# A Griffin-style encoder layer on one core: two score tiles of the short sequence in one PSUM buffer

## The chip, the cores and the metric

The kernel runs on one core of a Trainium2 chip. The metric is the device time of one launch, in microseconds (us), as the median of several runs. A core has five engines that run side by side: PE (TensorE, matrix multiplications; its weight loads are shown apart as PEld), DVE (VectorE), ACT (ScalarE), POOL (GpSimd) and SP (SyncE, which here only issues DMAs). PE writes its results to PSUM, a small memory of eight banks; a bank holds 512 fp32 numbers in each of 128 partitions, the output of one matmul of 512 columns. ACT and DVE read PSUM; POOL works on SBUF, the large working memory.

## The reference

One encoder layer is applied to two sequences with the same weights: `x_prompt` with 1024 tokens (the long sequence) and `x_sample` with 512 tokens (the short one). Cut to what matters here:

```python
z = xn @ w_in                          # xn = RMSNorm(x); split into q, k, v of A and B, two gates
# branch A: 8 query heads, 2 key/value heads, head width 64, every token sees every token
s = jnp.einsum('bqkgd,bskd->bkgqs', qi, k, preferred_element_type=jnp.float32) * scale
p = jax.nn.softmax(s, axis=-1)
o = jnp.einsum('bkgqs,bskd->bqkgd', p.astype(v.dtype), v)
# branch B: attention to a neighbourhood on a token grid, with a bias
merged = sigmoid(ga) * (o_a @ w_proj_a) + sigmoid(gb) * (o_b @ w_proj_b)
h = h + merged @ w_out
h = h + square(relu(RMSNorm(h) @ w_mlp_up)) @ w_mlp_down      # then a final RMSNorm
```

All of it is in fp32. The kernel keeps the precision by splitting a number into a high and a low part, each in a faster format of the matmul, and by adding two or three matmuls for one product.

## The kernel before

`run` does the token mixer of one sequence: first the short one (trunk 0, T = 512, NT = 4 blocks of 128 tokens, NB = 1 block of 512), then the long one (trunk 1, T = 1024, NB = 2). `mlp` then does the MLP for both. In the first 1050 us or so of the profile the mixers run, in the rest the MLP.

Branch A of a sequence is done in two passes, `g` = 0 and 1, one for each key/value head. In a pass, `phR` projects, normalises and rotates queries and keys (L630 to L711), and `phA` (L714 to L787) does the attention of four query heads. A *unit* of `phA` is one head and 512 queries; the short sequence has 4 units in a pass, and a unit has 4 score tiles j = 0 to 3 of 128 queries each. For one score tile, `s_tile` (L718)

- takes a PSUM buffer `s` (L723) and puts the scores into it: for each 512 keys one matmul with the keys' high part (L726) and one with the low part (L727);
- takes the negated maximum of each row on DVE (L729), and on ACT the exp of the scores with the row sum (L732): the last read of the PSUM buffer;
- divides: reciprocal on DVE (L734), scaling on POOL (L735).

The loop at L756 then goes through the key blocks kc = 0 to NT-1 of a unit: PE transposes the four tiles' probabilities of that key block into one PSUM bank (L769), ACT copies out the high part (L774), DVE makes the low part (L775), and two key blocks later PE multiplies with the values (`pv`, L745 and L746). The next unit's score tiles are written into the same loop: in the short sequence tiles 0 and 1 at kc = 0, tile 2 at kc = 1, tile 3 at kc = 2 (L777 to L780). `fill.pull` (L782) puts pieces of other work between: matmuls of the gate projection (`gate`, L409, through `mm3`, L190 to L193; tiles `gps`).

PSUM is shared by two pools. `pmm` has four buffers of one bank (`mm`, L93); `pbig` has two buffers of two banks each, 1024 columns (`big`, L96). Score tiles take `big` buffers. In the long sequence a score tile has 1024 columns and fills one; in the short sequence it has 512 columns, so `[:, :T]` uses one bank of the two. Other users of `big` are `transpose_tile` (L273: eight transposes into one buffer, L277; then for each of its two banks a copy on ACT, L287, and a subtraction on DVE, L293) and branch B's `s_unit` (L919). `s_unit` takes one buffer for two score tiles, one for each bank: for x = 0 and 1 two matmuls (L949), a reduction on DVE that reads the bank (L951), the exp on ACT (L955) and a scaling on POOL (L959).

All waits are set by the framework from what each instruction reads and writes and from when a buffer of a pool comes free. It also sets the order of the instructions on each engine, from its own plan of the run: earlier lines go first as far as they are planned to be ready, and operations marked `tc.keep_in_program_order` keep their place. So matmuls of `s_tile` and of the gate stand mixed on PE. On each engine the instructions then run in the order set.

Of the kernel before, what the change touches and what calls it, by code (L numbers as in the profile page):

```python
# [61 lines left out]
def encoder(ctx: ExitStack, tc: tile.TileContext, xs, outs, w):  # L62
# [21 lines left out]
    def phase(name, bufs=2):  # L84
        return tc.tile_pool(name=name, bufs=bufs, reuse_waits="tile")
# [7 lines left out]
    def mm(name):  # L93
        return pmm.tile([P, 512], F32, tag="mm", name=name)

    def big(name):  # L96
        return pbig.tile([P, 1024], F32, tag="big", name=name)
# [69 lines left out]
    def bias_row(r):  # L167
        nc.sync.dma_start(biases[r], shifted[:, :, 7 - r : 23 - r, :])
# [228 lines left out]
    def run(tr, nxt, first):  # L397
        N, x, T, NT, NB = tr.N, tr.x, tr.T, tr.NT, tr.NB
# [35 lines left out]
        def finish_o(o, n, dst, pool, nm):  # L434

            t = pool.tile([HD, 512], F32, tag="ot", name=f"ot_{nm}", bufs=1)
            nc.scalar.activation(t[:, :n], o[HD:P, :n], AF.Copy)
            b = pool.tile([HD, 512], F32, tag="os", name=f"os_{nm}", bufs=2)
            nc.vector.tensor_tensor(b[:, :n], o[0:HD, :n], t[:, :n], op=ALU.add)
            nc.scalar.dma_start(dst, b[:, :n])  # L440


        def load_a(g, between=None, then=None, last=None):
            wh, wl, rq = [], [], []
            for kb in range(2):
                wh.append(slot([P, 4, 384], F32R, f"wgh{N}_{g}_{kb}"))
                wl.append(slot([P, 4, 384], F32R, f"wgl{N}_{g}_{kb}"))
                raw = rawp.tile([P, 1024], F32, tag="raw", name=f"rawq{N}_{g}_{kb}")
                rv = raw.rearrange("p (k c) -> p k c", c=256)
                nc.sync.dma_start(  # L450
                    rv,
                    win[kb * 512 : (kb + 1) * 512, 256 * g : 256 * g + 256].rearrange("(k p) c -> p k c", p=P),
                )
                rq.append(rv)
            if between is not None:
                between()
            if then is None:
                for kb in range(2):
                    split(wh[kb][:, :, 0:256], wl[kb][:, :, 0:256], rq[kb])
            else:  # L460
                then([(wh[kb][:, :, 0:256], wl[kb][:, :, 0:256], rq[kb]) for kb in range(2)])
            raw = rawp.tile([P, 1024], F32, tag="raw", name=f"rawkv{N}_{g}")
            rv = raw.rearrange("p (k c) -> p k c", c=P)
            for i, off in enumerate((512 + 64 * g, 640 + 64 * g)):
                nc.sync.dma_start(
                    rv[:, :, 64 * i : 64 * i + 64],
                    win[:, off : off + 64].rearrange("(k p) c -> p k c", p=P),
                )
            if last is not None:
                last()  # L470
            for kb in range(2):
                split(
                    wh[kb][:, :, 256:384],
                    wl[kb][:, :, 256:384],
                    rv[:, kb * 4 : kb * 4 + 4, :],
                    between is not None,
                )
            return wh, wl

        def load_v(g, alloc, pin=False):  # L480
            return load_cols(win, 1792 + 256 * g, 256, f"v{N}_{g}", alloc, pin)

        early = {}
        for g in range(2):
            with phase(f"phR{N}_{g}") as ph:
# [122 lines left out]
                for tt in range(NT):  # L608
                    tb, j = divmod(tt, 4)
                    nm = f"{N}_{g}_{tt}"  # L610
# [103 lines left out]
            with phase(f"phA{N}_{g}") as ph:  # L714
                units = [(h, qb) for h in range(4) for qb in range(NB)]
                PP = {}

                def s_tile(u, j):  # L718
                    h, qb = u
                    nm = f"{N}_{g}_{h}_{qb}_{j}"  # L720
                    q0 = (qb * 4 + j) * P
                    lhs = qT[h % 2][:, h // 2, q0 : q0 + P]
                    s = big(f"s{nm}")[:, :T]  # L723
                    for kb in range(NB):
                        ks = slice(kb * 512, kb * 512 + 512)
                        nc.tensor.matmul(s[:, ks], lhs, kT[:, 0, ks], start=True, stop=False)  # L726
                        nc.tensor.matmul(s[:, ks], lhs, kT[:, 1, ks], start=False, stop=True)  # L727
                    nm_ = sml.tile([P, 1], F32, tag="nm", name=f"nm{nm}")
                    nc.vector.tensor_reduce(nm_, s, axis=AX.X, op=ALU.max, negate=True)  # L729
                    p = ph.tile([P, T], F32, tag="P", name=f"p{nm}", bufs=8)  # L730
                    l = sml.tile([P, 1], F32, tag="l", name=f"l{nm}")
                    nc.scalar.activation(p, s, AF.Exp, bias=nm_, accum_out=l)  # L732
                    rl = sml.tile([P, 1], F32, tag="rl", name=f"rl{nm}")
                    nc.vector.reciprocal(rl, l)  # L734
                    nc.gpsimd.tensor_scalar(p, p, rl, 1.0, op0=ALU.mult, op1=ALU.mult)  # L735
                    PP[u, j] = p

                o_of = {}

                def pv(u, kc, hi, lo):  # L740
                    h, qb = u
                    if kc == 0:
                        o_of[u] = mm(f"o{N}_{g}_{h}_{qb}")
                    o = o_of[u]
                    nc.tensor.matmul(o, vhl[:, kc, :], hi, start=(kc == 0), stop=False)  # L745
                    nc.tensor.matmul(o, vhl[:, kc, :], lo, start=False, stop=(kc == NT - 1))  # L746
                    if kc == NT - 1:
                        r0 = (g * 4 + h) * HD
                        finish_o(o, 512, oad[r0 : r0 + HD, qb * 512 : qb * 512 + 512], ph, f"A{N}_{g}_{h}_{qb}")

                for j in range(4):
                    s_tile(units[0], j)
                    fill.pull(2)
                queue = []
                LAG = 2
                for ui, u in enumerate(units):  # L756
                    h, qb = u
                    if first:
                        bias_row(g * 4 + ui)
                        if g == 0 and ui == 1:  # L760
                            early["a"] = load_a(1)
                        if g == 0 and ui == 2:
                            early["v"] = load_v(1, slot)
                    nxt_u = units[ui + 1] if ui + 1 < len(units) else None
                    sdone = 0
                    for kc in range(NT):
                        pt = mm(f"pT{N}_{g}_{h}_{qb}_{kc}")
                        for j in range(4):
                            nc.tensor.transpose(  # L769
                                pt[:, j * P : (j + 1) * P], PP[u, j][:, kc * P : (kc + 1) * P], ident  # L770
                            )
                        hi = ph.tile([P, 512], F32R, tag="pth", name=f"pth{N}_{g}_{h}_{qb}_{kc}", bufs=3)
                        lo = ph.tile([P, 512], F32R, tag="ptl", name=f"ptl{N}_{g}_{h}_{qb}_{kc}", bufs=3)
                        nc.scalar.activation(hi, pt, AF.Copy)  # L774
                        nc.vector.tensor_tensor(lo, pt, hi.bitcast(F32), op=ALU.subtract)  # L775
                        queue.append((u, kc, hi, lo))
                        if nxt_u is not None:  # L777
                            while sdone < 4 and kc >= ((0, 1, 3, 4) if NB == 2 else (0, 0, 1, 2))[sdone]:
                                s_tile(nxt_u, sdone)
                                sdone += 1  # L780

                        fill.pull(1 if NB == 1 or kc % 4 < 3 else 0)  # L782
                        if len(queue) > LAG:
                            pv(*queue.pop(0))
                fill.drain()
                for item in queue:
                    pv(*item)  # L787
# [55 lines left out]
        with phase(f"phB{N}") as ph:  # L843
# [210 lines left out]
            for i in range(n + LS + LV):  # L1054
                if NB == 1:
                    f = 9 if i < 1 else 5 if i < n - 4 else 6 if i < n else 4 if i == n else 2
                else:
                    f = 0 if i == n - 10 else 5 + (i % 3 > 0) if i < n - 8 else 7
# [37 lines left out]
        with phase(f"phG{N}") as ph:  # L1096
# [25 lines left out]
            for c in range(NC8):  # L1122
# [4 lines left out]
                for tb in range(NB):  # L1127
# [4 lines left out]
                    nm = f"{N}_{c}_{tb}"  # L1132
# [33 lines left out]
            for half in range(2):  # L1166
                wo = wos[half]
                hc = slice(half * 512, half * 512 + 512)
                for tt in range(NT):
                    tb, j = divmod(tt, 4)  # L1170
                    nm = f"{N}_{half}_{tt}"
# [61 lines left out]
                    if half == 1:  # L1233
# [5 lines left out]
                        if nxt is None:  # L1239
# [10 lines left out]
                            if 3 <= tt <= 5:  # L1250
                                j = tt - 3
# [556 lines left out]
    for i, tr in enumerate(trunks):  # L1808
        run(tr, trunks[i + 1] if i + 1 < len(trunks) else None, i == 0)
# [66 lines left out]
```

## Time and profile before

| what | us |
|---|---|
| median of 3 runs | 2132.78 (2132.7 to 2134.22) |
| the profiled execution | 2134.04 |
| its span, first to last instruction | 2132.2 |
| DVE busy | 1473.7 |
| ACT busy | 1114.3 |
| first pass of the short sequence's branch A, score tiles | 52.5 to about 85 |
| second pass, score tiles | 129 to about 161 |

A row of a group reads: line, engine, operation, tiles out<-in, shape, count, then times. Buffer numbers are left out of names, so `ss` is a score tile of branch A, `ps` its probabilities, `pTs` the transposed ones, `sbs` a score buffer of branch B, `ptxs` a buffer of transposed input, `gpss` a gate's sum. In the view of one tile, a row has the shortest, median and longest duration in ns, and the first and last start in us; below it stand the pauses by what ended them (us in total, times). In the timeline, the columns are start, duration, engine, line, operation and tiles; in brackets stands the idle time before it and who ended it. In the table by stretches, x counts instructions, and PEclk is PE's granted clock. A list of waits has engine, tile and line, then who was waited for: us in total, times, the longest.

### The profile page before, as it was taken

What the parts mean: (1) busy time and instruction counts of PE and PEld (TensorE: products, weight loads), DVE (VectorE), ACT (ScalarE), POOL (GpSimd) and SP (SyncE); (2) the same over time, 40 slices, a digit from 0 to 9 for tenths busy, and PEclk for the clock granted to TensorE, in tenths of its full rate; (3) what the DMA queues carried; (4) which work ended last, traced back from release to release, by engine and by line L of the source; (5) the groups of instructions that cost most, each with busy time, mean ns of one, the idle gap of its engine ahead of it and who ended that gap; (6) DMA issues with size and microseconds to landing.
All of it is one profiled execution on the core that took longest, in us unless ns stands there. A gap on an engine that the chain in (4) does not pass through costs nothing. (4 is left out here: it accounts for less than half of the span.)

```text
span 2132.2 us, 31826 instructions
## 1 busy us (share of the span) xinstructions
PE 2114.7 (99%) x10982; PEld 1849.5 (87%) x10982; DVE 1473.7 (69%) x2805; ACT 1114.3 (52%) x2345; POOL 388.2 (18%) x506
## 2 busy tenths in 40 slices
PE   9999999999999999999999999999999999999998
PEld 8888788988898888888888999999999988888887
DVE  6675686777667754656782977778777777759563
ACT  5654664556536644655531566566655643434352
POOL 2232420433233223433300200003000000000000
PEclk9999999999999999999999999999999999999999
DMA  6435567620221132433472666578445799688561
GB/s 187 130 105 171 156 187 242 195 72 30 62 83 53 43 108 85 123 106 108 138 247 101 212 200 193 161 249 210 158 145 159 255 351 341 220 275 281 172 197 70
DMA packets 319578, 350.91 MB, mean 165 GB/s; under 512 B 31160, under 2 KB 255032, under 8 KB 319417
## 3 DMA queue, kind: packets, MB, share of 16 engines
q1 hardware_dynamic: 278071, 279.91, 41.8%
q10 hardware_dynamic: 35666, 51.93, 7.0%
q0 software_dynamic: 5680, 17.04, 2.8%
q8 instruction: 87, 1.43, 0.3%
q14 instruction: 74, 0.61, 0.1%
HBM read 264.85 MB, written 87.88 MB: 165 GB/s over the span
## 5 line engine op out<-in xcount | busy, mean ns | idle before, releaser
L193 PE MATMUL dn<-wd,al 128*128 128x512 f32 (+1 forms) x624 | 242.4, 389 | 0.0
L192 PE MATMUL dn<-wd,ah 128*128 128x512 f32 (+1 forms) x624 | 242.4, 388 | 0.0
L191 PE MATMUL dn<-wd,ah 128*128 128x512 f32 (+1 forms) x624 | 242.4, 388 | 0.0
L1289 ACT ACTIVATE ah<-ar 128x512 fp32r<-128x512 f32 x168 | 104.4, 627 | 203.9 <-PE dn L192 183.3
L1290 DVE TENSOR_TENSOR al<-ar,ah 128x512 fp32r<-128x512 f32 x168 | 115.3, 693 | 77.5 <-ACT ah L1289 65.0
L193 PEld LDWEIGHTS dn<-wd,al 128*128 128x128 f32 x624 | 117.2, 188 | 24.2
L192 PEld LDWEIGHTS dn<-wd,ah 128*128 128x128 f32 x624 | 117.2, 188 | 24.1
L191 PEld LDWEIGHTS dn<-wd,ah 128*128 128x128 f32 x624 | 117.2, 188 | 24.0
L735 POOL TENSOR_SCALAR ps<-ps,rls 128x1024 f32<-128x1024 f32 (+1 forms) x96 | 96.8, 1010 | 215.7 <-DVE rls L734 201.3
L775 DVE TENSOR_TENSOR ptls<-pTs,pths 128x512 fp32r<-128x512 f32 x160 | 107.6, 686 | 37.8 <-ACT pths L774 37.1
L774 ACT ACTIVATE pths<-pTs 128x512 fp32r<-128x512 f32 x160 | 94.1, 598 | 73.7 <-PE pTs L769 71.7
L729 DVE TENSOR_REDUCE nms<-ss 128x1 f32<-128x1024 f32 (+1 forms) x96 | 99.8, 1041 | 24.9 <-PE ss L727 24.4
L176 POOL TENSOR_TENSOR rs_f<-ms_f,mhalf 128x1 f32<-128x1 f32 x6 | 4.0, 666 | 590.7 <-DVE ms_f L172 590.7
L732 ACT ACTIVATE ps<-ss,nms 128x1024 f32<-128x1024 f32 (+1 forms) x96 | 93.2, 972 | 23.8 <-DVE nms L729 19.8
L191 PE MATMUL gpss<-xs_0h,w_gs 128*128 128x512 f32 x256 | 104.7, 409 | 0.3 <-ACT w_gs L180 0.2
L769 PEld LDWEIGHTS pTs<-ident,ps 128*128 128x128 f32 x640 | 78.1, 140 | 28.2 <-POOL ps L735 4.1
L193 PE MATMUL gpss<-xs_0h,w_gs 128*128 128x512 f32 x256 | 101.0, 394 | 0.0
L192 PE MATMUL gpss<-xs_0l,w_gs 128*128 128x512 f32 x256 | 100.8, 394 | 0.0
L769 PE MATMUL pTs<-ident,ps 128*128 128x128 f32 x640 | 98.9, 274 | 1.2 <-DVE ptls L775 0.5
L1289 ACT ACTIVATE A<-S 128x512 fp32r<-128x512 f32 x128 | 76.0, 624 | 30.0 <-DVE S L1352 26.8
L1408 ACT ACTIVATE c<-c 128x384 f32<-128x384 f32 x97 | 50.8, 524 | 69.0 <-DVE c L1407 69.0
L1290 DVE TENSOR_TENSOR A<-S,A 128x512 fp32r<-128x512 f32 x128 | 84.4, 685 | 3.4 <-ACT A L1289 3.4
(344 smaller groups left out, 6402.3 us busy)
## 6 DMA issues: line engine op xcount, KB each, us to landing
ar<-ud SPq DMA_DIRECT2D x120, 512.0 KB
br<-in_w_mlp_down_dram SPq DMA_DIRECT2D x72, 512.0 KB
rawu<-in_w_mlp_up_dram SPq DMA_DIRECT2D x64, 512.0 KB
ud<-c ACTq DMA_DIRECT2D x128, 192.0 KB
raw_gs<-in_w_in_dram SPq DMA_DIRECT2D x32, 512.0 KB
zgs<-sgs ACTq DMA_DIRECT2D x48, 256.0 KB
ud<-cs SPq DMA_DIRECT2D x64, 192.0 KB
raw_os<-in_w_out_dram SPq DMA_DIRECT2D x16, 512.0 KB
```

The lines of the kernel that those rows point to most:

```text
L191: nc.tensor.matmul(out, ah, bh, start=start, stop=False, **kw)
L192: nc.tensor.matmul(out, ah, bl, start=False, stop=False, **kw)
L193: nc.tensor.matmul(out, al, bh, start=False, stop=stop, **kw)
L729: nc.vector.tensor_reduce(nm_, s, axis=AX.X, op=ALU.max, negate=True)
L732: nc.scalar.activation(p, s, AF.Exp, bias=nm_, accum_out=l)
L735: nc.gpsimd.tensor_scalar(p, p, rl, 1.0, op0=ALU.mult, op1=ALU.mult)
L769: nc.tensor.transpose(pt[:, j * P : (j + 1) * P], PP[u, j][:, kc * P : (kc + 1) * P], ident)
L774: nc.scalar.activation(hi, pt, AF.Copy)
L775: nc.vector.tensor_tensor(lo, pt, hi.bitcast(F32), op=ALU.subtract)
L1289: nc.scalar.activation(hi, src, AF.Copy)
L1290: nc.vector.tensor_tensor(lo, src, hi.bitcast(F32), op=ALU.subtract)
L1408: nc.scalar.activation(t, t, AF.Relu)
```

## The change

In branch A of the short sequence (NB = 2 is the long one) two successive score tiles share one buffer: the even tile takes a new `big` buffer and its first 512 columns, the odd one takes the second 512 columns of the same buffer. In the long sequence every tile still takes its own.

```diff
                 units = [(h, qb) for h in range(4) for qb in range(NB)]
                 PP = {}
+                pair = []
 
                 def s_tile(u, j):
...
                     lhs = qT[h % 2][:, h // 2, q0 : q0 + P]
-                    s = big(f"s{nm}")[:, :T]
+                    if NB == 2 or j % 2 == 0:
+                        pair[:] = [big(f"s{nm}")]
+                    s = pair[0][:, :T] if NB == 2 else pair[0][:, j % 2 * 512 : j % 2 * 512 + 512]
                     for kb in range(NB):
                         ks = slice(kb * 512, kb * 512 + 512)
                         nc.tensor.matmul(s[:, ks], lhs, kT[:, 0, ks], start=True, stop=False)
```

`ks` counts within `s`, so it is the same for both halves. The number of instructions of each kind stays as it is.

## The prediction

> **What bounds the kernel now.** I read the page first: the engines, then the chain that ended last.
>
> ```profile
> span 2132.2 us, 31826 instructions
> PE 2114.7 (99%) x10982; PEld 1849.5 (87%) x10982; DVE 1473.7 (69%) x2805; ACT 1114.3 (52%) x2345; POOL 388.2 (18%) x506
> ...
> PE 44%; DVE 0%; issue 0%; ACT 0%; POOLq 0%; POOL 0%; DVEq 0%; ACTq 0%
> ```
>
> PE (matmuls) is busy for 2114.7 of 2132.2 us, and the chain is PE alone. The change removes no matmul, so it can act only through time in which PE stands still: 2132.2 - 2114.7 = 17.5 us in the whole span. How much of it lies where the change is made? The table by stretches has the short sequence's branch A, first pass (52 to 97) and second pass (128 to 170).
>
> ```profile
> core 0: us, PE busy (x) PEld busy (x) DVE busy (x) ACT busy (x) POOL busy (x), PEclk, DMA share, GB/s
> 52.00:97.00 45.00, 43.97 (x219) 34.13 (x218) 33.72 (x69) 31.40 (x66) 11.88 (x16) 1.00 0.46 141
> ...
> 128.00:170.00 42.00, 41.46 (x211) 32.61 (x210) 30.93 (x63) 28.32 (x62) 12.07 (x17) 1.00 0.42 117
> ```
>
> PE is idle there for 1.03 + 0.54 = 1.6 us. Next, the view of the score tile `ss` up to 230 us: its instructions, and the pauses that ended at them or because of them.
>
> ```profile
> L726 PE MATMUL ss<-kTs,qTs x32: 389/476/505, 52.5 to 158.1; 128*128 128x512 f32 x32
> ...
> L729 DVE TENSOR_REDUCE nms<-ss x32: 671/691/693, 54.4 to 159.3; 128x1 f32<-128x512 f32 x32
> L732 ACT ACTIVATE ps<-ss,nms x32: 676/687/705, 55.3 to 160.2; 128x512 f32<-128x512 f32 x32
> ...
>   ACT ps L732: 2.3, 5
> ...
>   PEld ss L726: 1.7, 4
>   PE ss L726: 0.6, 1
> ```
>
> There are 32 score tiles. Their matmuls waited for an exp (L732) five times, 2.3 us in all: 1.7 us is idle time of the weight loader (PEld), 0.6 us of PE itself. That is the wait for a free score buffer. The timeline shows the largest one:
>
> ```profile
> 82.16 0.19 PEld L726 LDWEIGHTS ss<-kTs,qTs 128*128 128x128 f32 x1 [0.81 <-ACT ps L732]
> 82.16 0.50 PE L726 MATMUL ss<-kTs,qTs 128*128 128x512 f32 x1 [0.58 <-ACT ps L732]
> ```
>
> **Removed: the wait for a buffer.** Today tile j of a unit takes the buffer of tile j-2 and waits for that tile's exp. With pairs, tiles 0 and 1 lie in one buffer, 2 and 3 in the other, and a pair takes the buffer of the pair before last, whose exps are a unit old. The five waits go: between 0.6 us (PE's own idle time) and 2.3 us (the loader's added). Does anything take their place?
>
> **Added: tile 1 behind tile 0.** The two halves are different banks, but they are one tile to whoever sets the waits. The kernel already has such a layout: branch B's `s_unit` puts two scores into the two banks of one buffer (L949), each read by a reduction on DVE (L951). The second score reads nothing that the first one's reduction makes, so if waits went by bank, it would not wait. The first and the last of the 48 units, in the timeline:
>
> ```profile
> 184.67 0.42 DVE L951 CUSTOM_DVE_ANT_0 sbss<-sbs,bms 128x256 f32<-128x256 f32 x1 [0.59 <-issue]
> 185.02 0.08 DVE L951 DVE_READ_ACCUMULATOR2_ANT msbs<- 128x1 f32 x1
> 185.16 0.30 PEld L949 LDWEIGHTS sbs<-kBs,qBs 128*128 128x128 f32 x2 [0.37 <-DVE msbs L951]
> 185.16 0.51 PE L949 MATMUL sbs<-kBs,qBs 128*128 128x256 f32 x2
> ...
> 1043.96 0.56 DVE L951 CUSTOM_DVE_ANT_0 sbss<-sbs,bms 128x384 f32<-128x384 f32 x1 [0.30 <-PE sbs L949]
> 1044.44 0.08 DVE L951 DVE_READ_ACCUMULATOR2_ANT msbs<- 128x1 f32 x1
> ...
> 1044.58 0.30 PEld L949 LDWEIGHTS sbs<-kBs,qBs 128*128 128x128 f32 x2 [0.17 <-DVE msbs L951]
> ```
>
> The second score's matmuls start 0.06 us (185.16 - 185.10) or more after the first one's reduction has ended. So it is in 44 of the 48 units; in the other four two scores go out ahead of a reduction, as two units' first scores may, and never more than two. A second place says the same. In `transpose_tile` eight transposes fill a buffer, four to a bank:
>
> ```profile
> 8.58 1.11 PE L277 MATMUL ptxs<-ident,xns 128*128 128x128 f32 x4
> 9.91 1.06 PE L277 MATMUL ptxs<-ident,xns 128*128 128x128 f32 x4
> 11.01 1.09 ACT L287 ACTIVATE xs_0h<-ptxs 128x512 fp32r<-128x512 f32 x2 [2.32 <-PE ptxs L277]
> 12.13 0.69 DVE L293 TENSOR_TENSOR xs_0l<-ptxs,xs_0h 128x512 fp32r<-128x512 f32 x1 [2.72 <-ACT xs_0h L287]
> ```
>
> The first bank is full at 9.69; ACT, idle for 2.32 us, starts reading it at 11.01, when the second bank is full too (10.97). So I take waits to go by tile: after the change tile 1 waits for tile 0's exp, and tile 3 for tile 2's. How long that is, the timeline shows for one tile:
>
> ```profile
> 56.65 0.39 PE L726 MATMUL ss<-kTs,qTs 128*128 128x512 f32 x1
> 56.88 0.39 PE L727 MATMUL ss<-kTs,qTs 128*128 128x512 f32 x1
> 57.30 0.69 DVE L729 TENSOR_REDUCE nms<-ss 128x1 f32<-128x512 f32 x1 [0.38 <-PE ss L727]
> 58.03 0.69 ACT L732 ACTIVATE ps<-ss,nms 128x512 f32<-128x512 f32 x1 [1.30 <-DVE nms L729]
> 58.62 0.19 ACT L732 ACTIVATION_READ_ACCUMULATOR ps<-ss,nms 128x1 f32 x1
> ```
>
> From first matmul to last read: 58.81 - 56.65 = 2.2 us. That is the same chain as today, and there are as many links: two per unit inside it (before, 0 to 2 and 1 to 3; after, 0 to 1 and 2 to 3) and two to the next unit. In the opening of a pass tiles 0 and 2 go out first in place of 0 and 1, and the four exps end when they do now. What changes is how near in the program a link's ends lie. `s_tile` is called at key blocks 0, 0, 1, 2: today's links span one and two key blocks, the new ones none and one. So each of the 16 odd tiles (2 passes x 4 heads x 2) becomes a close link, behind which PE's whole queue stands: the gate matmuls, the transposes (L769), the value products (L745, L746).
>
> **The price of a close link.** No row shows it for branch A, so I bound it by branch B's:
>
> ```profile
> PE sbs L949 <- DVE msbs L951: 1.3, 4, 0.4
> ...
> PEld sbs L949 <- DVE msbs L951: 11.7, 37, 0.9
> ```
>
> By PE's own idle time it is 1.3 / 48 = 0.03 us per link, by both together 13.0 / 48 = 0.27 us; for 16 tiles 0.4 or 4.3 us. Less what is removed, by the same two measures: 0.4 - 0.6 = -0.2 us, or 4.3 - 2.3 = +2.0 us. Idle time of the loader is partly covered by the matmul still running; one row of a close link shows both:
>
> ```profile
> 190.27 0.30 PEld L949 LDWEIGHTS sbs<-kBs,qBs 128*128 128x128 f32 x2 [0.63 <-DVE msbs L951]
> 190.27 0.51 PE L949 MATMUL sbs<-kBs,qBs 128*128 128x256 f32 x2 [0.20 <-DVE msbs L951]
> ```
>
> 0.20 of 0.63, about a third, reaches PE. Counting a third of the loader's pauses (my choice, from this row): added (1.3 + 11.7/3) / 48 x 16 = 1.7 us, removed 0.6 + 1.7/3 = 1.2 us; net **+0.5 us**.
>
> **What hides a later score.** The next unit's first transposes need all four of its probabilities, the last one after POOL's scaling:
>
> ```profile
> 66.90 0.69 POOL L735 TENSOR_SCALAR ps<-ps,rls 128x512 f32<-128x512 f32 x1 [0.33 <-DVE rls L734]
> ...
> 67.58 0.60 PE L769 MATMUL pTs<-ident,ps 128*128 128x128 f32 x4
> ```
>
> They start just as that ends (67.59), so a later tile 3 delays the unit. PE meanwhile does gate matmuls, which have to be done anyway:
>
> ```profile
> L191 PE MATMUL gpss<-xs_0h,w_gs x26: 388/392/475, 51.9 to 90.1; 128*128 128x512 f32 x26
> ```
>
> They last until 90.1 of a pass that ends near 95, and behind them the next pass' projections are ready. I cost the delay at nothing. If the gate matmuls ran out early, the delay itself would show on PE (second rival).
>
> **Sum.** 2134.04 us (the profiled execution; 1.84 us lie around its span) + 0.5 = 2134.5. That execution is 1.3 us above the median of the runs, 2132.78, so the forecast for the median is **2133.3 us**: no change that can be told, since about 0.2%, 4.3 us, is the least that a measurement of this kernel tells from none.
>
> **Rivals.** *Waits go by bank.* Then tile 1 is free at once, the buffer waits go and nothing comes: 2132.78 - 1.2 = 2131.6, at best 2132.78 - 2.3 = 2130.5; still within 0.2%. Against it stand branch B's units and the transposes; for it only that branch B's reader is another instruction than an exp. The Trainium skill ("PSUM — Partial Sum Buffer", "PSUM bank collisions raise a hardware error") has PSUM guarded by bank and quadrant, not by the whole buffer; by that rule tile 1 would need no wait, and the two places above do not agree with it. Chance 0.06.
>
> *Every odd tile stops PE.* Tile 1 is ready in the plan just when tile 0's exp is planned to end; if DVE or ACT is late in fact, PE stops as at 82.16, for 0.58 us, in both passes. 16 x 0.58 = 9.3, less 0.6: +8.7 us, 2141.5. It is over 0.2% from (4.3 + 0.6) / 16 = 0.31 us of PE idle per odd tile. For it: the two links of a unit are closer than today's. Against it: branch B's 48 close links cost 0.03 us of PE each. Chance 0.08, of which 0.07 over 0.2%.
>
> *The order elsewhere shifts.* The order on each engine is planned as a whole, so scores that stand elsewhere may move waits in later stages. Between those stages and now lie 17.5 - 1.6 = 15.9 us of PE idle; a third of it more or less is 5 us (an estimate), 2127.5 to 2138.1. Nothing in the profile points to a side. Chance 0.13: 0.04 faster by over 0.2%, 0.05 within, 0.04 slower.
>
> *The change does nothing at all:* tiles 1 and 2 merely trade places, and the time stays at 2132.8; this lies inside the forecast's case.
>
> **Numbers.** The forecast has 0.73: its bounds are 2132.6 to 2134.8. Range for 8 in 10: 2130.5 (waits by bank at best) to 2136.5 (odd tiles at 0.27 us of PE each: 4.3 - 0.6 = +3.7). Faster by over 0.2%: 0.04, and 0.01 taken from the forecast for what I overlook, 0.05. Slower: 0.07 + 0.04 = 0.11. Same: 0.72 + 0.06 + 0.01 + 0.05 = 0.84.
>
> **What would show it.** In the profile after, in each unit tile 2's first matmul should stand before tile 1's, tile 1's matmul just behind tile 0's exp; idle before L726 put down to the exp should be near 16 x 0.27 = 4 us, mostly PEld's; PE idle in the two passes near 2 us; PE's busy time unchanged. Two scores back to back in one buffer would show waits by bank; over 5 us of PE idle in front of L726 the second rival; equal passes and another time, the third.

## The result, and the profile after

The changed kernel takes 2137.42 us (median of 18 runs, 2135.74 to 2138.33), the kernel before 2133.25 us (18 runs, 2132.43 to 2134.84): a ratio of 1.0019, 95% interval 1.0013 to 1.0025. It is 4.2 us slower, 0.9 us above the top of the predicted range. The profiled execution took 2138.22 us. Its page, with the span, the busy times and the chain:

```profile
span 2135.9 us, 31820 instructions
...
PE 2116.1 (99%) x10982; PEld 1848.8 (87%) x10982; DVE 1474.8 (69%) x2805; ACT 1115.8 (52%) x2345; POOL 389.7 (18%) x506
...
PE 81%; DVE 2%; DMA 2%; issue 1%; ACT 1%; POOL 1%; SPq 0%; ACTq 0%; POOLq 0%; DVEq 0%
```

The span grew by 3.7 us, PE's idle time from 17.5 to 19.8 us. The lines of `phA` have moved down by three: L726 is now L729, the maximum L732, the exp L735, the scaling L738, the value products L748 and L749, the transposes L772, the low part L778.

Where does the time go? A good gauge is an instruction that has the same matmuls in front of it in both kernels. Branch B's first score, right behind the second pass, is one. In the view of its tile `sbs`, the first start stands after the durations; before and after:

```profile
L949 PE MATMUL sbs<-kBs,qBs x64: 279/285/391, 182.7 to 295.3; 128*128 128x256 f32 x64
```

```profile
L952 PE MATMUL sbs<-kBs,qBs x64: 279/284/391, 186.2 to 298.7; 128*128 128x256 f32 x64
```

3.5 us of the 3.7 us are lost by then. 1.1 us of them are lost in the first pass: the matmuls `zs` behind it begin at 94.4 before and at 95.5 after. The table by stretches, from branch A's first score to branch B's first, has the same work in both kernels (the counts differ by one at the edge); before and after:

```profile
52.53:182.72 130.19, 128.62 (x688) 107.16 (x687) 85.17 (x196) 75.19 (x192) 37.76 (x53) 1.00 0.44 132
```

```profile
52.49:186.22 133.73, 130.15 (x687) 106.82 (x686) 86.17 (x196) 75.99 (x192) 38.83 (x53) 1.00 0.43 129
```

PE is idle there for 1.6 us before and 3.6 us after. The other 1.5 us of the loss stand in PE's busy time, though the matmuls are the same. A matmul's row reaches into the next one: rows of 0.39 us start 0.23 us apart. So a pause of up to 0.16 us between two of them does not show as idle time. What holds PE? The view of the score tile `ss` up to 230 us, after:

```profile
L729 PE MATMUL ss<-kTs,qTs x32: 389/476/501, 52.5 to 161.3; 128*128 128x512 f32 x32
...
  DVE nms L732: 13.9, 12
  PE ss L730: 7.7, 9
  ACT ps L735: 0.8, 4
...
  PEld ss L729: 0.8, 4
```

The scores themselves stop PE less than before: pauses behind an exp are 0.8 us (four times, the weight loader alone) instead of 2.3. What has grown is ACT's idle time before an exp, waiting for a maximum: 13.9 us against 5.4 (`DVE nms L729: 5.4, 8` before). The maxima come late. The opening of the first pass, in the timeline of after (the other work of PE left out), shows how:

```profile
55.24 0.69 ACT L735 ACTIVATE ps<-ss,nms 128x512 f32<-128x512 f32 x1 [0.40 <-DVE nms L732]
55.43 0.39 PE L729 MATMUL ss<-kTs,qTs 128*128 128x512 f32 x1
...
55.65 0.39 PE L730 MATMUL ss<-kTs,qTs 128*128 128x512 f32 x1
...
56.56 0.39 PE L729 MATMUL ss<-kTs,qTs 128*128 128x512 f32 x1
...
56.79 0.39 PE L730 MATMUL ss<-kTs,qTs 128*128 128x512 f32 x1
...
57.21 1.29 DVE L732 TENSOR_REDUCE nms<-ss 128x1 f32<-128x512 f32 x2 [1.00 <-PE ss L730]
...
57.94 0.69 ACT L735 ACTIVATE ps<-ss,nms 128x512 f32<-128x512 f32 x1 [1.92 <-DVE nms L732]
```

At 55.24 tile 0's exp starts. At 55.43 PE writes tile 2, complete at 56.04. At 56.56, behind tile 0's exp, it writes tile 1, complete at 57.18. DVE has stood idle for 1.00 us, although tile 2 has been ready since 56.04, because its own order is still 0, 1, 2, 3: tile 1's maximum stands in front. It then does both in one stretch (x2, 1.29 us); ACT, in the same order, idles for 1.92 us. PE's order is now 0, 2, 1, 3 and the readers' is 0, 1, 2, 3: the orders *cross*, and tile 2 waits 1.78 us for nothing that it needs. It is so in every unit of both passes. At three of the six changes of unit, moreover, the next unit's tile 0 goes out ahead of tile 3 (its first matmul at 59.08 against 59.44, 74.94 against 78.03, 137.22 against 137.57), which crosses the orders once more. Summed over the 32 tiles, the time from the end of a score's second matmul to the start of its maximum is 11.9 us before and 31.2 us after. Unit 0's last exp starts at 60.93, against 59.16.

How that reaches PE, the second pass shows in one place:

```profile
158.91 1.26 DVE L732 TENSOR_REDUCE nms<-ss 128x1 f32<-128x512 f32 x2
...
160.09 1.27 DVE L778 TENSOR_TENSOR ptls<-pTs,pths 128x512 fp32r<-128x512 f32 x2
...
160.91 0.63 PE L772 MATMUL pTs<-ident,ps 128*128 128x128 f32 x4 [1.03 <-DVE ptls L778]
```

The maxima of tiles 1 and 2 of the last unit come as one block at 158.91. The low parts stand behind them on DVE, and PE's next transposes wait 1.03 us for the first low part, the last reader of a bank of `pmm`. By lines, from 45 to 180 us (busy time, mean ns, then idle time before and what ended it), before:

```profile
L191 PE MATMUL gpss<-xs_0h,w_gs 128*128 128x512 f32 x64 | 25.9, 404 | 0.1
...
L769 PE MATMUL pTs<-ident,ps 128*128 128x128 f32 x128 | 21.0, 276 | 0.7 <-POOL ps L735 0.3 <-DVE ptls L775 0.2
L726 PE MATMUL ss<-kTs,qTs 128*128 128x512 f32 x32 | 14.4, 451 | 0.7 <-ACT ps L732 0.6
```

and after:

```profile
L191 PE MATMUL gpss<-xs_0h,w_gs 128*128 128x512 f32 x64 | 26.1, 408 | 1.0 <-ACT sgs L430 1.0
...
L772 PE MATMUL pTs<-ident,ps 128*128 128x128 f32 x128 | 22.4, 277 | 2.1 <-DVE ptls L778 1.0 <-POOL ps L738 0.4 <-DVE os_As L439 0.2
L729 PE MATMUL ss<-kTs,qTs 128*128 128x512 f32 x32 | 14.3, 455 | 0.0
...
L748 PE MATMUL os<-pths,vhls 128*128 128x512 f32 x32 | 13.1, 409 | 0.4 <-DVE ptls L778 0.4
```

The idle time in front of scores (0.7 us) is gone. In its place stand 2.1 us in front of transposes, 1.0 us in front of gate matmuls (which wait for the gate's sigmoid on ACT, `sgs`), and 0.4 us in front of value products. That is the idle time alone. Counted from the start of a matmul to the start of the next, and compared with the usual step of its kind (the median before), all of the 3.5 us show: 2.0 us more in front of transposes, 1.2 us of value products, 1.2 us of gate matmuls and 0.2 us of the next projection's transposes, 1.0 us less in front of scores.

### The profile page after: what moved, and what is told of

Same layout as the page of the kernel before. It is cut to its first block, busy times and chain, and to the rows that moved or that the text cites. A ratio compares the mean times of both kernels' runs of the same rounds, so it can differ in the third digit from the quotient of the medians.

```text
span 2135.9 us, 31820 instructions
## 1 busy us (share of the span) xinstructions
PE 2116.1 (99%) x10982; PEld 1848.8 (87%) x10982; DVE 1474.8 (69%) x2805; ACT 1115.8 (52%) x2345; POOL 389.7 (18%) x506
## 4 chain that ended last, share of the span: by engine, by line
PE 81%; DVE 2%; DMA 2%; issue 1%; ACT 1%; POOL 1%; SPq 0%; ACTq 0%; POOLq 0%; DVEq 0%
PE dn L191 7%; PE dn L192 7%; PE dn L193 7%; PE pTs L772 3%; PE gpss L191 3%; PE gpss L193 3%; PE gpss L192 2%; PE ud L191 2%; PE uc L191 2%; PE ud L192 2%; PE uc L192 2%; PE uc L193 2%; PE ud L193 2%; PE ua L191 2%; PE ua L192 2%; PE ua L193 2%
## 5 line engine op out<-in xcount | busy, mean ns | idle before, releaser
L738 POOL TENSOR_SCALAR ps<-ps,rls 128x1024 f32<-128x1024 f32 (+1 forms) x96 | 96.6, 1007 | 221.7 <-DVE rls L737 214.4
L778 DVE TENSOR_TENSOR ptls<-pTs,pths 128x512 fp32r<-128x512 f32 x160 | 107.3, 686 | 37.9 <-ACT pths L777 37.4
L732 DVE TENSOR_REDUCE nms<-ss 128x1 f32<-128x1024 f32 (+1 forms) x96 | 99.4, 1040 | 23.5 <-PE ss L730 22.8
L735 ACT ACTIVATE ps<-ss,nms 128x1024 f32<-128x1024 f32 (+1 forms) x96 | 93.2, 972 | 31.4 <-DVE nms L732 28.9
L772 PEld LDWEIGHTS pTs<-ident,ps 128*128 128x128 f32 x640 | 78.0, 140 | 30.9 <-POOL ps L738 5.7
L772 PE MATMUL pTs<-ident,ps 128*128 128x128 f32 x640 | 100.3, 274 | 2.6 <-DVE ptls L778 1.4
```

The lines of the kernel that those rows point to most:

```text
L772: nc.tensor.transpose(pt[:, j * P : (j + 1) * P], PP[u, j][:, kc * P : (kc + 1) * P], ident)
```

## The experiments

The theory to be tested: **crossed orders**. The tile-level wait makes the plan put tile 2's matmuls ahead of tile 1's, while DVE and ACT keep the order of the program; a score that is ready stands behind one that isn't, the unit's probabilities come later, and PE pays downstream. The rivals: the **close link** (PE itself loses at the wait of tile 1 for tile 0's exp), and the **sharing** itself (that two tiles lie in one buffer, whatever the orders). All kernels were timed in five rounds against the kernel before on the same chip. As 1 to 2 us of a single profile also come from later stages, the table has the time that the profile shows for the two passes, from the first score of branch A to the first score of branch B (130.2 us before).

| kernel | orders cross | median us (before) | ratio, 95% interval | two passes, us |
|---|---|---|---|---|
| the changed kernel | all 8 units | 2137.42 (2133.25) | 1.0019 [1.0013, 1.0025] | +3.5 |
| calls 0, 2, 1, 3 | none | 2134.13 (2133.69) | 1.0000 [0.9991, 1.0009] | +0.3 |
| readers 0, 2, 1, 3 | 2 units | 2136.36 (2133.69) | 1.0012 [1.0003, 1.0021] | +1.3 |
| own buffers, PE crossed | all 8 | 2137.35 (2133.69) | 1.0017 [1.0008, 1.0026] | +2.7 |
| own buffers, readers crossed | all 8 | 2136.30 (2134.17) | 1.0011 [1.0003, 1.0020] | +2.1 |
| sharing in the first pass only | 4 units | 2135.62 (2134.17) | 1.0007 [0.9999, 1.0016] | +1.3 |
| sharing in the second pass only | 4 units | 2135.76 (2134.17) | 1.0007 [0.9998, 1.0016] | +1.6 |
| last tile first | all 8 | 2138.28 (2133.65) | 1.0022 [1.0013, 1.0031] | +5.2 |
| torn on purpose | none | 2133.03 (2133.65) | 0.9996 [0.9987, 1.0005] | -0.5 |

**The sharing kept, the orders made to agree.** The changed kernel, with `s_tile` called for tiles 0, 2, 1, 3; the pairs 0 and 1, 2 and 3 still share.

```diff
-                for j in range(4):
+                CALLS = (0, 2, 1, 3) if NB == 1 else (0, 1, 2, 3)
+                for j in CALLS:
...
-                                s_tile(nxt_u, sdone)
+                                s_tile(nxt_u, CALLS[sdone])
```

> The changed kernel with the tiles of the short sequence called in the order 0, 2, 1, 3; tiles 0 and 1 still share a buffer, 2 and 3 the other. Main theory (queue order): PE writes the scores in the order 0, 2, 1, 3 because tile 1 waits for the exp of tile 0, while DVE and ACT read them in the order 0, 1, 2, 3, so tile 2 stands in PSUM until tile 1 is through; here all three engines have the order 0, 2, 1, 3, and the time goes back to that of before, 2133.3 us within 1 us. Rival link (PE loses at each close wait of tile 1 for tile 0): the wait spans two calls here, as before the change, so 2133.3 us too. Rival sharing (matmuls into one bank of a buffer and reads of its other bank slow each other): nothing is changed, 2137.4 us.

2134.13 us: no loss that can be told, and 0.3 us in the two passes. In its timeline the readers take tile 2 at once:

```profile
54.74 0.40 PE L730 MATMUL ss<-kTs,qTs 128*128 128x512 f32 x1
55.17 0.69 DVE L732 TENSOR_REDUCE nms<-ss 128x1 f32<-128x512 f32 x1 [0.16 <-PE ss L730]
...
55.90 0.69 ACT L735 ACTIVATE ps<-ss,nms 128x512 f32<-128x512 f32 x1
...
56.59 0.39 PE L729 MATMUL ss<-kTs,qTs 128*128 128x512 f32 x1
```

The maximum of 55.17 is tile 2's, 0.03 us behind its second matmul, and the waits from matmul to maximum are back at 12.0 us. The two tiles still share, and tile 1's matmuls (56.59) still come behind tile 0's exp, but nothing is lost. So sharing costs nothing by itself. The waits keep a matmul into one bank of a buffer and a read of its other bank apart here, so what those two would cost each other side by side, no run shows. Nor does this run part the crossing from the close link: with the calls 0, 2, 1, 3 the link lies two calls apart again, as in the kernel before.

**The link kept, the readers' order changed.** `s_tile` is cut in two, the matmuls (`s_mm`) and the readers (`s_rest`). Only the readers of tile 1 are written behind those of tile 2; its matmuls keep their place in the program.

```diff
+                def s_call(u, j):
+                    if NB == 1 and j == 1:
+                        late.append(partial(s_rest, u, j, *s_mm(u, j)))
+                        return
+                    s_tile(u, j)
+                    while late:
+                        late.pop()()
```

> The changed kernel with tile 1's matmuls where they are and only its reads (maximum, exp, scaling) written behind those of tile 2. PE keeps the order 0, 2, 1, 3 and the close wait of tile 1 for the exp of tile 0; DVE and ACT get 0, 2, 1, 3. Queue order: 2133.3 to 2134.5 us. Rival link: 2137 us, as the wait of PE is kept. Rival sharing: 2137.4 us.

About two thirds of the loss in the two passes is gone (1.3 us left of 3.5), the median less: 2136.36 lies above the range expected, and its interval overlaps that of the changed kernel, so by the median alone the two cannot be told apart (the profile puts a further 1.3 us into later stages). The plan of PE came out partly otherwise than meant: in the third unit of each pass tile 1 is complete ahead of tile 2 again. So two of the eight units cross the other way round, and the timeline shows the first of them:

```profile
70.52 0.62 PE L733 MATMUL ss<-kTs,qTs 128*128 128x512 f32 x2
...
71.19 0.69 DVE L738 TENSOR_REDUCE nms<-ss 128x1 f32<-128x512 f32 x1 [0.88 <-PE ss L733]
...
74.87 0.67 DVE L738 TENSOR_REDUCE nms<-ss 128x1 f32<-128x512 f32 x1
```

Tile 1, complete at 70.92, has its maximum at 74.87, behind tile 2's and other work of DVE. What is left of the loss may be those two units or the close link; this run does not part them.

**No sharing, PE's order crossed by hand.** The kernel before with a buffer for each tile; only tile 2's matmuls are written ahead of tile 1's.

```diff
+                    if NB == 1 and j == 1:
+                        late.append(partial(s_rest, u, 2, *s_mm(u, 2)))
+                    if NB == 1 and j == 2:
+                        late.pop()()
+                    else:
+                        s_tile(u, j)
```

> The kernel before, each tile with a buffer of its own, but tile 2's matmuls written ahead of tile 1's, so that PE has 0, 2, 1, 3 and tile 1 takes tile 0's buffer behind its exp, while DVE and ACT read 0, 1, 2, 3. Queue order: the loss of the change without any shared buffer, 2136.5 to 2138 us, and maxima of tile 2 that start 1.5 us or more behind its matmuls. Rival link: 2136 to 2138 us too, since tile 1 waits for the exp of tile 0 here as well. Rival sharing: 2133.3 us.

2137.35 us, about the loss of the change (2.7 us in the two passes, against 3.5), without a shared buffer. The opening looks as in the changed kernel, the maxima joined into one block and ACT idle for 1.95 us:

```profile
54.88 0.39 PE L730 MATMUL ss<-kTs,qTs 128*128 128x512 f32 x1
...
56.72 0.39 PE L729 MATMUL ss<-kTs,qTs 128*128 128x512 f32 x1
...
57.37 1.29 DVE L735 TENSOR_REDUCE nms<-ss 128x1 f32<-128x512 f32 x2 [1.03 <-PE ss L730]
58.10 0.69 ACT L738 ACTIVATE ps<-ss,nms 128x512 f32<-128x512 f32 x1 [1.95 <-DVE nms L735]
```

The rival of sharing falls. The link is not excluded here: tile 1 takes the buffer of tile 0 and waits for its exp too.

**No sharing, the readers crossed.** The mirror image: PE's order stays 0, 1, 2, 3, and the readers of tile 1 come behind those of tile 2, in the kernel before. Tile 1 has a buffer of its own and doesn't wait for tile 0.

```diff
+                    if NB == 1 and j == 1:
+                        late.append(partial(s_rest, u, j, *s_mm(u, j)))
+                        return
```

> The kernel before with a buffer for each tile as it was and TensorE's order 0, 1, 2, 3 kept, but the maximum and the exp of tile 1 are written behind those of tile 2, so that VectorE and ScalarE go 0, 2, 1, 3. The crossing is the same as in the changed kernel, mirrored, and nothing is shared. Theory of the crossed orders: tile 2's readers stand ahead of tile 1's, tile 1's score waits for them, the unit's exps end later, and the two passes lose 1.5 to 3 us at equal TensorE work; time 2135 to 2137. Rival, the close link on TensorE from the exp of one tile to the matmuls of its neighbour: here no tile shares a buffer, so nothing of the loss is there; 2133 to 2134.

2136.30 us, 2.1 us above before, and 2.1 us in the two passes: the crossing costs time from the other side as well. By the rival it would have been 2133 to 2134. One link did move: tile 3 now takes tile 2's buffer and waits for its exp, in place of tile 1's. But the scores' pauses behind an exp are 1.2 us here (four times, the loader alone), fewer than the 2.3 us before, so the loss does not lie in such waits.

```profile
54.30 0.39 PE L730 MATMUL ss<-kTs,qTs 128*128 128x512 f32 x1
...
56.36 0.39 PE L730 MATMUL ss<-kTs,qTs 128*128 128x512 f32 x1
56.79 1.29 DVE L735 TENSOR_REDUCE nms<-ss 128x1 f32<-128x512 f32 x2 [1.03 <-PE ss L730]
57.52 0.69 ACT L738 ACTIVATE ps<-ss,nms 128x512 f32<-128x512 f32 x1 [1.95 <-DVE nms L735]
```

Here tile 1, complete at 54.69, stands behind tile 2, complete at 56.75.

**One pass at a time.**

```diff
-                    if NB == 2 or j % 2 == 0:
+                    if NB == 2 or g != 0 or j % 2 == 0:
```

> The changed kernel with the sharing in the first of the two passes alone; the second pass has a buffer for each tile. Both theories put the loss where the sharing is: from the changed kernel's trace 1.1 to 1.3 us at the end of the first pass, and nothing more in the second; time 2134.5, give or take 1 for later stages. If the second pass lost its 2.2 us all the same, the loss would not come from the sharing in that pass but from something handed on by the first.

(and with `g != 1`)

> The changed kernel with the sharing in the second of the two passes alone. Expected: nothing lost at the end of the first pass, 2.2 us at the end of the second; time 2135.5, give or take 1 for later stages. If the loss of the second pass were handed on from the first, it would be under 1 us here, 2134 or less.

+1.3 and +1.6 us in the passes; together 2.9 of the changed kernel's 3.5 us. In the traces the loss arises in each pass by itself and isn't handed on. The medians (1.5 and 1.6 us) fit, but each interval takes in 1. The second pass lost somewhat less than the 2.2 us expected.

**Torn transposes: a theory that fell.** In the changed kernel a key block's four transposes often don't go together: the program's order on PE has the short sequence's 128 transposes in 47 runs, 18 of them single, against 38 and 5 before, and their busy time rose from 21.0 to 22.4 us. Was the tearing the cost? Two kernels ask: one tears them in the kernel before, the other lets the changed kernel begin each key block with tile 3, the last to come.

```diff
                             nc.tensor.transpose(
...
+                            if NB == 1 and j == 0:
+                                fill.pull(1)
...
-                        fill.pull(1 if NB == 1 or kc % 4 < 3 else 0)
+                        fill.pull(1 if NB == 2 and kc % 4 < 3 else 0)
```

> The kernel before, with each key block's four transposes torn apart on purpose: the piece of gate work that the program put behind them is put behind the first of them. Score buffers, scores, maxima and exps are as before. In the order of TensorE the short sequence's 128 transposes then go in 51 runs, 19 of them single, against 38 and 5 in the kernel before, 47 and 18 in the changed kernel, where their busy time is 22.4 us against 21.0. Theory that torn transposes are how the late probabilities cost TensorE time: busy time of the transposes near 22.5 us, 1 to 2 us lost in the two passes, 2134.5 to 2136. If only the waits behind late probabilities count, not the tearing: 2133 to 2134.

```diff
-                        for j in range(4):
+                        for j in (3, 0, 1, 2) if NB == 1 else range(4):
```

> The changed kernel, sharing and crossed orders kept, but each key block's transposes begin with tile 3, the one whose probabilities come last; the other three are planned behind it, and none goes ahead alone (29 runs, 2 of them single). If the tearing carries part of the loss: transposes busy for 20 to 21 us, as before or less, and the loss of 3.5 us in the two passes falls to 1 to 2 us, 2134 to 2136. If the lateness of the last probability itself is what stalls TensorE, however the transposes stand: the loss stays at 3 us or grows, 2136.5 or more.

The groups of the transposes, first torn on purpose, then with the last tile first:

```profile
L769 PE MATMUL pTs<-ident,ps 128*128 128x128 f32 x128 | 22.8, 273 | 0.4 <-POOL ps L735 0.4
```

```profile
L772 PE MATMUL pTs<-ident,ps 128*128 128x128 f32 x128 | 20.4, 289 | 1.4 <-POOL ps L738 1.0 <-DVE ptls L778 0.3
```

With 51 runs and 22.8 us busy the first kernel loses nothing (2133.03 us); with 29 runs and 20.4 us the second still loses 4.6 us. The tearing is a mark of late probabilities, not the cost. PE does other work between torn transposes, and busy time that grows need not be lost time. In the last kernel every group waits for the probabilities that are latest, and the two passes lose 5.2 us. That fits lateness as the cost, but it doesn't show each step from there to PE: of its idle time only 1.4 us stand in front of transposes, 1.2 in front of value products (for low parts) and 1.1 in front of the next projection's transposes.

**Buffers of one bank.** If two tiles in one buffer bring waits that need not be, the same eight banks can be cut otherwise: four buffers of one bank each while the scores are one bank wide. Tried in the short sequence's branch A, in branch B of both sequences, and in both places. In the edit `four[0]` is the pool of these four banks; it is closed at the border of such a stretch and opened anew with the other size of buffer (not shown).

```diff
+    def one(name):
+        return four[0].tile([P, 512], F32, tag="one", name=name)
...
-                    s = big(f"s{nm}")[:, :T]
+                    s = big(f"s{nm}") if NB == 2 else one(f"s{nm}")
...
-                    so = s[:, x * 512 : x * 512 + nkey]
+                    so = one(f"sb{nm}")[:, :nkey]
```

In branch A alone:

> The kernel before with four buffers of one bank each for the score tiles of the short sequence's branch A (the two buffers of two banks are given up for that phase and come back behind it): the same four banks, but waits of each tile for itself. Queue order and link: no tile waits for another one of its unit, all engines have the order 0, 1, 2, 3, and the buffer waits of before are gone too: 2131 to 2133 us. Rival sharing: 2131 to 2133 us. If giving up and taking back the pool makes waits of its own at the phase's ends, up to 1 us more.

2133.09 us against 2133.69, a ratio of 0.9998 [0.9989, 1.0007]: it can't be told from before, though branch B's first score starts at 181.8, 0.9 us earlier.

In branch B alone:

> The candidate's second half alone: four buffers of one bank in the attention of branch B of both sequences, branch A of the short sequence as in the kernel before. In the candidate's profile TensorE stood 1.2 us ahead of the kernel before at the end of the short sequence's second pass, a further 2.4 us at the end of its branch B, and 2.6 us ahead of it at the end. If the close links of branch B cost what they show, this kernel is 1 to 3 us faster than before: 2131 to 2133. If the candidate's 2.3 us came from branch A alone, it is at the time before, 2133.3 to 2134.5.

2133.19 us against 2133.47, 0.9998 [0.9989, 1.0007]: less than expected.

In both, twice:

> The candidate against both: the kernel before with the same eight banks, but four buffers of one bank each in the places where scores are one bank wide, in the short sequence's branch A and in the attention of branch B of both sequences (there two tiles share a buffer in the kernel before, 48 units). Every score waits then for its own tile four scores back, the orders of TensorE, VectorE and ScalarE agree, and the close links of branch B are gone. Theory of the crossed orders: branch A gains 0 to 1 us as four one-bank buffers alone did (0.9 us at equal TensorE work); branch B, whose close links cost TensorE an estimated 3.7 us from start to start, gains at most that; time 2129 to 2133. If sharing costs nothing in branch B, since no orders cross there, 2133 to 2134.

> The candidate once more, for its interval: the first five rounds gave a ratio of 0.9993 with one as its upper bound inside the interval. Expected 2131.5 to 2133 and a ratio of 0.9985 to 0.9995; with a ratio above 0.9998 the candidate cannot be told from the kernel before.

2131.91 us against 2134.17, 0.9993 [0.9984, 1.0002], and 2131.46 against 2133.47, 0.9992 [0.9984, 1.0001]. Each interval takes in 1; the two together (their mean, and 0.0009 / √2 as half width) give 0.99925 ± 0.0006, about 1.6 us less than before, give or take 1.3. So it has the lowest medians of the study, by little. Its list of PEld's waits for `sbs` (branch B alone has the same two rows, as L959):

```profile
PEld sbs L964 <- ACT kBs L925: 0.7, 2, 0.3
PEld sbs L964 <- DVE kBs L927: 0.7, 3, 0.3
```

The 11.7 us for the reductions on DVE are gone from both lists, and PE's 1.3 us too. Of these 13.0 us, 2.3 us at most came back as time where branch B alone was changed (the lower end of its interval, 0.9989), which bounds what 48 close links cost.

## Why the prediction was wrong

*What bounds the kernel.* Right: PE at 99%, and only its idle time counts; that grew.

*Removed: the wait for a buffer.* Right: the pauses behind an exp fell from 2.3 to 0.8 us, and PE's own idle time in front of scores from 0.7 us (0.6 of it for an exp) to 0.0.

*Added: tile 1 behind tile 0.* Right in the mechanism: tile 2's matmuls stand before tile 1's, and tile 1's start behind the exp of tile 0, by 0.05 to 0.54 us in the eight units. The rival that waits go by bank did not come: the two tiles lie in different banks, and in all eight units tile 1 comes behind tile 0's exp. The Trainium skill's guard by bank and quadrant ("PSUM — Partial Sum Buffer", "PSUM bank collisions raise a hardware error") is not what sets these waits.

*The step that failed* is the sentence "That is the same chain as today, and there are as many links", with "the four exps end when they do now". The links were counted on PE alone. PE's order became 0, 2, 1, 3, but DVE's and ACT's stayed 0, 1, 2, 3, and their part in the chain was left out. So the first unit's exps do not end when they did: the last starts 1.8 us later (60.93 against 59.16). With the calls 0, 2, 1, 3 all orders agree, the links lie two calls apart, and nothing is lost (2134.13 against 2133.69). With the readers' order alone put right in six of eight units, 1.3 of the 3.5 us are left in the two passes.

*The price of a close link.* The forecast took +0.5 us net from branch B's links, and the profile was to show close to 4 us of pauses behind an exp. It shows 0.8: as a price of the link the sum was even too high. But branch B's orders don't cross, so its rows could not hold the cost that came.

*What hides a later score.* Failed too: "I cost the delay at nothing." The gate matmuls did not run out, yet the delay reached PE in front of transposes (2.1 us), gate matmuls (1.0) and value products (0.4), since on DVE and ACT the low parts and the sigmoids queue behind maxima and exps that come late and in blocks. The text named the sign to look for, that the delay would show on PE, but tied it to one condition that wasn't needed.

*The rivals.* "Every odd tile stops PE" had the right sign and the wrong place: PE doesn't stop at odd tiles. "The order elsewhere shifts" is not what happened: 3.5 of the 3.7 us are lost before branch B. (Single profiles of other kernels differ by 1 to 2 us behind that point, but runs of one kernel also differ by 2.4 us, 2132.43 to 2134.84.)

*What can be told.* The 0.2% taken as the least difference that can be told was too coarse: with 18 runs of each kernel the interval is 0.06% to either side.

*What stays open:* how much of the 3.5 us the close link takes. The crossing without that link costs 2.1 us, though it is the mirror image and not the same crossing. With the link and six of eight units uncrossed 1.3 us are left, so by these single traces the link takes at most about that.

## What to carry to other kernels

When a change moves one engine's work within its order, look at the orders of the engines that read it: if these don't move along, a result that is ready waits behind one that isn't, and the delay shows where no one looks for it, here at transposes and gate matmuls. Before two tiles share a buffer, ask who waits on the whole buffer; then either issue the tiles so that the partners lie two steps apart, which cost nothing here, or cut the memory into buffers of the size that is used. And compare two profiles at an instruction with the same work in front of it: that shows in one number where a loss of 0.2% arises.

## What was not expected of the hardware

A busy share is not a measure of loss even on an engine that is busy for 99%: the 128 transposes were busy for 22.8 us in a kernel that lost nothing and for 20.4 us in one that lost 4.6 us. Two tiles in the two banks of one buffer cost nothing as such (2134.13 us with all pairs shared and the orders in agreement, against 2133.69): what cost time was the order that their wait brought about.
